# First layer's down projection in four pairs of column chunks, nine seven-product couples each, with GpSimd making the weights' sums

## The chip, the cores and the metric

The kernel runs on one core of a Trainium2 chip. The metric is device time in microseconds: 2390.53 us, the median of 3 runs (2390.34 to 2392.72). Engines are named as in the profile: PE (TensorE matmuls), PEld (its weight loads), DVE (VectorE), ACT (ScalarE), POOL (GpSimd), SP (SyncE, whose queue issues nearly all DMAs).

## The reference

A two-layer encoder over 256 tokens of width 2048. Each layer is a token mixer and then a gated MLP; each has an RMS norm ahead of it and is added to the residual. All is float32.

```python
h = x
for layer in range(2):
    h = h + mixer[layer](rmsnorm(h, g_mix[layer]))          # mLSTM, then HGRN2
    h = h + conv_glu(rmsnorm(h, g_ffn[layer]), ...)
return rmsnorm(h, final_g)

def conv_glu(hn, w_up, conv_w, conv_b, w_down):
    a, v = jnp.split(hn @ w_up, 2, axis=-1)                 # 2048 -> 2 x 5504
    c = conv_b + sum(pad(a)[:, j:j + s] * conv_w[j] for j in range(3))
    return (gelu(c) * v) @ w_down                           # 5504 -> 2048
```

The change is in the last line, `@ w_down`: 43 tiles of 128 rows (k-tiles) times 2048 columns, for 256 tokens.

## The kernel before

**Precision.** Each float32 operand is split into a rounded part (ACT casts, L137) and a rest (DVE subtracts, L138), and a product of two blocks is three matmuls: high by high, high by low, low by high (`product`, L234).

**The order.** One list of chunks is worked through by `stream`. `split_weights` yields pieces of split weights, three ahead of the matmuls (`LOOK`). Raw weights arrive in three buffers of 1 MB (`RAW`), split ones lie in four (`WB`). A scheduler with a timeline of its own then orders the instructions of each engine; DMAs sent through `late` stay in program order on SP's queue. `side` runs small jobs beside the matmuls, by a count of modelled time (`side.tick`).

**The MLP** (`ffn`) has two parts: 22 k-tiles (FA) and 21 (FB). For each, the up projection is computed first, a chunk of 256 columns per k-tile, and then the down projection of these k-tiles. The 2048 output columns are four chunks of 512. In the first part they go as two pairs of chunks (`pair`, `squares_by_seven`); in the second as one pair (chunks 0, 1) and two ordinary chunks (2, 3; `project`, weights w_d2).

**Couples.** Inside a pair, two k-tiles form a couple: a 2 x 2 block product (token halves by k-tiles, k-tiles by column chunks). An ordinary couple takes 8 block products, 24 matmuls. A seven-product couple (in `SEVEN`) takes 7, or 21 matmuls, by Strassen's scheme in Winograd's form. It needs sums of the tokens, S1 to S4 (`token_sums`, four DVE additions and a split), and sums of the weights, T1 to T4 (`weight_sums`, L174 to 184, one DVE operation of 1024 columns and two of 512). A layer has 7 + 6 + 6 of these couples. The products of all couples collect in eight PSUM banks. After the last seven-product couple `mid` adds four of them to the residual `hm` (six DVE operations, one ACT, two POOL: L553 and L554); after the last couple `done` adds the others.

**Sums made ahead.** For six couples of each pair (`STORED`) the T's are made during the up projection: `prepare` (L573) loads two blocks of 512 KB into the tiles `th` and `tl` (shown as pth, ptl), DVE makes the sums, and two stores of 512 KB put them into a DRAM scratch (`tscr`). In the down projection `split_squares` (L186) loads 768 KB of raw weights (B11, B22, B21) and the two sums (1 MB) and splits all: ACT casts (L137, L209) and DVE subtracts (L138, L210), three of 1024 columns and one of 512. Each high or low part of the T's has one buffer.

Of the kernel before, what the change touches and what calls it, by code (L numbers as in the profile page):

```python
# [8 lines left out]
F32 = mybir.dt.float32  # L9
# [39 lines left out]
SEVEN = (1, 2, 4, 5, 7, 8, 9), (1, 2, 4, 5, 7, 8), (1, 2, 4, 5, 7, 8)  # L49
STORED = (1, 2, 4, 5, 7, 8)  # L50
# [10 lines left out]
def trunk_kernel(ctx, tc, xT, x_d, fg_d, pp_d, cst_d, w_gate, w_first, w_aq, w_ak, w_av, w_ao, w_aout, w_ao2,  # L61
                 w_bq, w_bv, w_bg, w_bout, w_bo2, w_up, w_d0, w_d1, w_d2, out, mscr, tscr):
# [113 lines left out]
    def weight_sums(a, b, T, T_):  # L176

        B22, B21, B12 = a[:, 512:1024], b[:, 0:512], b[:, 512:1024]
        dve.tensor_tensor(T.rearrange("p (a b) -> p a b", a=2), B12.unsqueeze(1).broadcast_to([P, 2, 512]),
                          a.rearrange("p (a b) -> p a b", a=2), ALU.subtract)  # L180
        yield 2.5
        dve.tensor_tensor(T_[:, 0:512], B22, T[:, 0:512], ALU.subtract)
        yield 2.5
        dve.tensor_tensor(T_[:, 512:1024], B21, T_[:, 0:512], ALU.subtract)

    def split_squares(ch, parts):  # L186
# [4 lines left out]
        def raw(u):  # L191
            if u not in raws and u < units:
                raws[u] = load_raw(ch.src, 2048 * u, min(2048 * (u + 1), 1024 * ch.nk) - (512 if u in ch.stored else 0))
                if u in ch.stored:
                    kept[u] = [temporary(ch.pool, "T") for _ in range(2)]
                    for t, src in zip(kept[u], ch.stored[u]):
                        nc.sync.dma_start(t, src)
            return raws.get(u)

        def combine(u):  # L200
            r = raw(u)
            T, T_ = kept[u] if u in kept else (temporary(ch.pool, "T") for _ in range(2))
            if u not in kept:
                for _ in weight_sums(r[:, 0:1024], r[:, 1024:2048], T, T_):
                    pass
# [7 lines left out]
        for u in range(units):  # L213
            r = raw(u)
            if u + 1 in ch.seven and not ch.late:
                combine(u + 1)
            wh, wl = parts(r[:, 0:1024], 1024)
            yield wh, wl, 1
            if u + 1 in ch.seven and ch.late:
                combine(u + 1)  # L220
            if 2 * u + 1 < ch.nk:
                m = 512 if u in ch.seven else 1024
                wh, wl = parts(r[:, 1024:1024 + m], m)
                yield wh, wl, sums.pop(u, None)

    def squares_by_seven(ch, fetch, ready):
# [20 lines left out]
        for u in range(units):  # L247
# [3 lines left out]
            if 2 * u + 1 == ch.nk:  # L251
                x = ch.x(2 * u)
                for ps, t, w in ((C11, 0, 0), (C12, 0, 1), (C21, 1, 0), (C22, 1, 1)):
                    product(ps, half(x, t), block(p[:2], w), True)
                side.tick(2.7)
                break
            fetch()
            q = ready.pop(0)
            x0, x1 = ch.x(2 * u), ch.x(2 * u + 1)
            A11, A21, A12, A22 = half(x0, 0), half(x0, 1), half(x1, 0), half(x1, 1)  # L260
            B11, B22, B21 = block(p[:2], 0), block(p[:2], 1), block(q[:2], 0)
            if u in ch.seven:
                sx, t = ch.sums(u), q[2]
                S1, S3, S2, S4 = ((sx[:, i * P:(i + 1) * P], sx[:, 512 + i * P:512 + (i + 1) * P]) for i in range(4))
                T1, T3, T2, T4 = (block(t[i // 2], i % 2) for i in range(4))
                for i, (ps, x, w) in enumerate(((P1, A11, B11), (C12, S4, B22), (C11, A12, B21), (P5, S1, T1),
                                                (P7, S3, T3), (P6, S2, T2), (C21, A22, T4))):
                    product(ps, x, w, u == last and ps in psm_)
                    side.tick(0.65)
# [4 lines left out]
            for ps, (x, w), (y, v) in ((C11, (A11, B11), (A12, B21)), (C12, (A11, B12), (A12, B22)),  # L274
                                       (C21, (A21, B11), (A22, B21)), (C22, (A21, B12), (A22, B22))):
# [251 lines left out]
    def token_sums(mp, i, a, b, S):  # L527

        sx = mp.tile([P, 1024], F32R, tag=f"sx{i}", name="sx")
# [3 lines left out]
        act.copy(sx[:, 0:512], S)  # L533
        dve.tensor_tensor(sx[:, 512:1024], S, sx[:, 0:512].bitcast(F32), ALU.subtract)
        return sx

    def pair(src, nk, c0, x, sums, norm, seven, late=False):
# [18 lines left out]
        def done(ps):  # L556
            for i in range(4):
                h = part(i // 2, i % 2)
                dve.tensor_tensor(h, h, ps[i], ALU.add)
            if norm is not None:  # L560
                norm.add(c0)
# [11 lines left out]
    def prepare(mp, todo, period, finished):  # L573

        yield 24.0
        for src, dst in todo:
            r, T = ([mp.tile([P, 1024], F32, tag=f"{n}{i}", name=f"p{n}") for i in range(2)] for n in ("th", "tl"))
            for i in range(2):
                late(r[i], src[:, i * 1024:(i + 1) * 1024])
            yield 9.0  # L580
            yield from weight_sums(*r, *T)
            for i in range(2):
                nc.sync.dma_start(dst[i], T[i])
            yield max(1.0, period - 14.0)
# [512 lines left out]
    def ffn(layer, norm, nxt):  # L1097
        stack = ExitStack()
        box = dict(n=3 * len(STORED) * layer)
# [10 lines left out]
        def done_up(f, i, GT, SX, seven):  # L1110
            def go(ps):
# [15 lines left out]
                if i % 2 and i // 2 in seven:  # L1127
                    SX[i // 2] = token_sums(mp, seven.index(i // 2), box["c"], c, avc[:, 0:2 * T])
# [3 lines left out]
        for part, (f0, nf) in enumerate(((0, FA), (FA, FB))):  # L1132
            GT, SX, todo, finished = [], {}, [], []

            def prep(todo=todo, finished=finished, nf=nf):
                if not pairs[0].pool:
                    begin()
                side.push(prepare(box["mp"], todo, (nf * 10.4 - 24.0) / len(todo) - 1.5, finished))

            for i in range(nf):  # L1140
                chunks.append(Chunk("fm", w_up[layer, f0 + i], KT, norm.x, done_up(f0 + i, i, GT, SX, SEVEN[2 * part]),
                                    prep if i == 0 else None,
                                    swap=(2,) if part and i == 0 else (3,) if f0 + i == 1 else (), paced=True))
            def two(src, c0, norm, seven, GT=GT, SX=SX, nf=nf, todo=todo, finished=finished):
                ch = pair(src, nf, c0, lambda k: GT[k], lambda u: SX[u], norm, seven)
                for u in STORED:
# [141 lines left out]
```

## Time and profile before

| | us |
|---|---|
| runs, median of 3 | 2390.53 |
| span of the profiled execution | 2388.5 |
| PE busy | 2372.4 |
| DVE busy | 1944.1 |
| ACT busy | 1298.8 |
| POOL busy | 189.7 |
| moved by DMA | 555.07 MB, mean 232 GB/s |

The profiled execution is one run; its span, first to last instruction, is 2.0 us shorter than the median of the runs. "Busy" for PE overlaps: a matmul starts before the one ahead has ended, so the price of one is read from a row of many. Stages, by the trace: the first layer's first up projection from about 388 to 632 us, two pairs to 745, the second up projection to 978, a pair and two chunks to about 1100, the second mixer to about 1680; the second layer's MLP from there to the end.

### The profile page before, as it was taken

The page shows a single profiled execution, that of the slowest core. Times are in us where ns is not written, and L with a number is a line of the kernel's source. Part 1 is how long each engine was busy: PE and PEld are TensorE (multiplying, and loading weights), DVE is VectorE, ACT ScalarE, POOL GpSimd, SP SyncE. Part 2 cuts the span into 40 slices and gives each one's busy share as a digit, 9 for nine tenths or more (in the row PEclk, how much of TensorE's full clock was granted, in tenths as well). Part 3 has the DMA queues.
Part 4 walks back from the last instruction along what each step waited for, and adds up shares of the span by engine and source line. Part 5 has one row for each costly group of instructions (what it writes and reads, how often), then busy time and mean ns, then how long its engine had stood idle before and what let it go on. Part 6 is the DMA issues. An engine that isn't in the chain of part 4 may idle for free.

```text
span 2388.5 us, 37988 instructions
## 1 busy us (share of the span) xinstructions
PE 2372.4 (99%) x14614; PEld 2030.4 (85%) x14614; DVE 1944.1 (81%) x3221; ACT 1298.8 (54%) x2013; POOL 189.7 (8%) x240
## 2 busy tenths in 40 slices
PE   9999999999999999999999999999999999999998
PEld 7888888888888888888888888888888888888887
DVE  7766687988887888777888888888889888788874
ACT  7655455454564554555555555555555565454563
POOL 0100000000000000001222222220000000000000
PEclk9999999999999999999999999999999999999999
DMA  8654556988787777755554554545798888677774
GB/s 300 201 180 165 183 178 211 333 294 317 269 293 254 251 239 262 273 194 182 173 171 168 175 177 160 177 166 188 258 325 298 298 281 296 231 249 263 249 266 148
DMA packets 98789, 555.07 MB, mean 232 GB/s; under 512 B 11168, under 2 KB 11680, under 8 KB 50736
## 3 DMA queue, kind: packets, MB, share of 16 engines
q1 hardware_dynamic: 96912, 548.64, 65.6%
q0 software_dynamic: 1120, 3.21, 0.7%
q8 instruction: 114, 1.87, 0.3%
q10 hardware_dynamic: 576, 0.79, 0.1%
q14 instruction: 67, 0.55, 0.1%
HBM read 512.69 MB, written 39.91 MB: 231 GB/s over the span
## 4 chain that ended last, share of the span: by engine, by line
PE 98%; DVE 1%; issue 1%; DMA 0%; ACT 0%; SPq 0%; POOLq 0%; POOL 0%
PE mm L328 37%; PE mm L344 23%; PE mm L332 18%; PE pc L237 12%; PE mm L237 5%; PE pn L776 1%; PE py L1034 1%; PE pd L984 1%; PE pz L405 0%; PE pa L984 0%; DMA raw<-in_w_first 0%; PE S L762 0%; DVE tl L210 0%; PE pz L1055 0%; PE pa L1009 0%
## 5 line engine op out<-in xcount | busy, mean ns | idle before, releaser
L328 PE MATMUL mm<-xt,wh 128*128 128x512 f32 x3776 | 1313.4, 394 | 0.0
L137 ACT CAST wh<-raw 128x1024 fp32r<-128x1024 f32 (+1 forms) x846 | 853.5, 1019 | 693.8 <-PE mm L328 237.9
L138 DVE TENSOR_TENSOR wl<-raw,wh 128x1024 fp32r<-128x1024 f32 (+1 forms) x846 | 1004.7, 1195 | 265.1 <-ACT wh L137 257.6
L332 PE MATMUL mm<-xt,wl 128*128 128x256 f32 x3776 | 1045.9, 278 | 0.0
L328 PEld LDWEIGHTS mm<-xt,wh 128*128 128x128 f32 x3776 | 706.2, 188 | 159.4
L332 PEld LDWEIGHTS mm<-xt,wl 128*128 128x128 f32 x3776 | 709.5, 188 | 4.5 <-issue 0.4
L344 PE MATMUL mm<-wh,xt 128*128 128x512 f32 x1024 | 320.5, 391 | 3.0 <-ACT xt L350 1.3
L344 PEld LDWEIGHTS mm<-wh,xt 128*128 128x128 f32 x1024 | 191.4, 188 | 43.3 <-ACT xt L350 1.7
L344 PE MATMUL mm<-wl,xt 128*128 128x512 f32 x512 | 198.2, 391 | 0.0
L237 PE MATMUL pc<-wh,g 128*128 128x512 f32 x508 | 167.2, 389 | 0.0
L355 ACT COPY b<-mm 128x256 f32<-128x256 f32 x236 | 87.4, 370 | 122.9 <-PE mm L332 122.7
L210 DVE TENSOR_TENSOR tl<-T,th 128x1024 fp32r<-128x1024 f32 x88 | 109.9, 1264 | 38.9 <-ACT th L209 36.7
L209 ACT CAST th<-T 128x1024 fp32r<-128x1024 f32 x88 | 92.7, 1054 | 73.6 <-PE mm L237 43.5
L237 PEld LDWEIGHTS pc<-wh,g 128*128 128x128 f32 x508 | 95.4, 188 | 19.9
L344 PEld LDWEIGHTS mm<-wl,xt 128*128 128x128 f32 x512 | 96.2, 188 | 18.9
L553 POOL TENSOR_TENSOR hm<-hm,u 128x512 f32<-128x512 f32 x8 | 10.4, 1302 | 1150.9 <-DVE u L552 1150.9
L237 PE MATMUL pc<-wl,g 128*128 128x512 f32 x254 | 98.9, 389 | 0.0
L344 PE MATMUL mm<-wh,g 128*128 128x512 f32 x308 | 96.6, 392 | 0.0
L237 PE MATMUL mm<-th,sx 128*128 128x512 f32 x264 | 91.9, 390 | 0.0
L356 DVE TENSOR_TENSOR avc<-mm,b 128x256 f32<-128x256 f32 x172 | 72.0, 418 | 14.7 <-ACT b L355 14.7
L361 DVE TENSOR_TENSOR avc<-avc,R 128x256 f32<-128x256 f32 x172 | 71.9, 419 | 1.6
L976 DVE COPY kq<-QK 128x256 f32<-128x256 f32 x224 | 69.7, 336 | 0.0
(260 smaller groups left out, 2476.7 us busy)
## 6 DMA issues: line engine op xcount, KB each, us to landing
raw<-in_w_up SPq DMA_DIRECT2D x172, 1024.0 KB, 5.5
raw<-in_w_d SPq DMA_DIRECT2D x48, 1024.0 KB, 5.0
raw<-in_w_bq SPq DMA_DIRECT2D x48, 1024.0 KB, 4.9
pth<-in_w_d SPq DMA_DIRECT2D x72, 512.0 KB, 6.7
tscr<-ptl SPq DMA_DIRECT2D x72, 512.0 KB, 4.7
T<-tscr SPq DMA_DIRECT2D x72, 512.0 KB, 5.1
raw<-in_w_d SPq DMA_DIRECT2D x36, 768.0 KB, 5.2
raw<-in_w_ao SPq DMA_DIRECT2D x24, 1024.0 KB, 4.8
```

Of the source, the lines that this page charges most:

```text
L137: pin(act.copy(wh[:, :m], r))
L138: pin(dve.tensor_tensor(wl[:, :m], r, wh[:, :m].bitcast(F32), ALU.subtract))
L209: act.copy(th, t)
L210: dve.tensor_tensor(tl, t, th.bitcast(F32), ALU.subtract)
L237: pe.matmul(ps, a, b, start=id(ps) not in begun, stop=stop and i == 2)
L328: pe.matmul(ps[f], wh[:, c:c + P], x, start=k + kk == 0, stop=False)
L332: pe.matmul(ps[f][:, 0:T], wl[:, c:c + P], x[:, 0:T], start=False, stop=k + kk == ch.nk - 1)
L344: pe.matmul(ps[t], x[:, a + t * P:a + (t + 1) * P], w[:, c], start=st and i == 0, stop=sp and i == 2)
L355: act.copy(b, ps[:, T:2 * T])
L356: dve.tensor_tensor(dst, ps[:, 0:T], b, ALU.add)
L361: dve.tensor_tensor(dst, dst, R, ALU.mult)
L976: dve.tensor_copy(m[:, j].rearrange("k (m p j) -> k m p j", p=2, j=h), blocks(z, h, 0, T))
```

## The change

- The first layer's chunks 2 and 3 of the second part become a pair too (weights w_d3 in the pair's layout). The second layer keeps its two ordinary chunks there.
- Seven-product couples: nine in each of the first layer's four pairs (couples 1 to 9), 9, 9 and 7 in the second layer's three: 36 + 25 instead of 19 + 19.
- `prepare` now makes T1, T2 and T3 in place on POOL, three operations of 512 columns, from three of the four blocks (512 KB and 256 KB); it stores 512 KB and 256 KB. All seven-product couples of the MLP are prepared.
- T4 is made in the down projection: POOL subtracts T2 from B21, ACT casts, POOL makes the low part. T3 is loaded beside B21 into the raw buffer, so that one split covers both.
- The products of such a couple are issued as four pieces of 2, 2, 2 and 1 products instead of two pieces.
- `token_sums` casts and splits S4 apart from the rest; in the pairs with nine couples it takes the place of token half 2 of the couple's first k-tile, which a seven-product couple doesn't read.
- In ordinary couples C21 comes before C12; `done` closes column chunk by column chunk.

```diff
-SEVEN = (1, 2, 4, 5, 7, 8, 9), (1, 2, 4, 5, 7, 8), (1, 2, 4, 5, 7, 8)
-STORED = (1, 2, 4, 5, 7, 8)
+SEVEN = tuple(range(1, 10)), (1, 2, 3, 5, 6, 7, 8)
...
+                n = 1536 if u in ch.stored else min(2048, 1024 * ch.nk - 2048 * u)
+                raws[u] = load_raw(ch.src, 2048 * u, 2048 * u + n)
                 if u in ch.stored:
-                    kept[u] = [temporary(ch.pool, "T") for _ in range(2)]
-                    for t, src in zip(kept[u], ch.stored[u]):
-                        nc.sync.dma_start(t, src)
+                    kept[u] = temporary(ch.pool, "T")
+                    nc.sync.dma_start(kept[u], ch.stored[u][:, 0:1024])
+                    nc.sync.dma_start(raws[u][:, 1536:2048], ch.stored[u][:, 1024:1536])
...
+            if u in ch.stored:
+                T4 = ch.pool.tile([P, 512], F32, tag="t4", name="t4")
+                pool.tensor_tensor(T4, r[:, 1024:1536], kept[u][:, 512:1024], ALU.subtract)
             wh, wl = parts(r[:, 0:1024], 1024)
             yield wh, wl, 1
+            if u in ch.stored:
+                th, tl = (ch.pool.tile([P, 1024], F32R, tag=n, name=n) for n in ("th0", "tl0"))
+                act.copy(th, kept[u])
+                dve.tensor_tensor(tl, kept[u], th.bitcast(F32), ALU.subtract)
+                yield th, tl, 0
...
+            if u in ch.stored:
+                th, tl = (ch.pool.tile([P, 512], F32R, tag=n, name=n) for n in ("th1", "tl1"))
+                act.copy(th, T4)
+                pool.tensor_tensor(tl, T4, th.bitcast(F32), ALU.subtract)
+                yield th, tl, 0
...
+            if u in ch.stored:
+                S1, S3, S2, S4 = ch.sums(u)
+                products((P1, A11, B11), (C12, S4, B22))
+                fetch()
+                t = ready.pop(0)
+                products((P5, S1, block(t[:2], 0)), (P6, S2, block(t[:2], 1)))
+                fetch()
+                q = ready.pop(0)
+                products((C11, A12, block(q[:2], 0)), (P7, S3, block(q[:2], 1)))
+                fetch()
+                t = ready.pop(0)
+                products((C21, A22, t[:2]))
...
     def prepare(mp, todo, period, finished):
...
+        yield 20.0
+        load(0)
+        for i, (_, dst) in enumerate(todo):
+            yield period / 2
+            r, b = loaded[i]
+            for out, x, y in ((r[:, 0:512], b, r[:, 0:512]), (b, b, r[:, 512:1024]), (r[:, 512:1024], r[:, 512:1024], r[:, 0:512])):
+                pool.tensor_tensor(out, x, y, ALU.subtract)
+            yield period / 4
+            load(i + 1)
+            yield period / 4
+            nc.sync.dma_start(dst[:, 0:1024], r)
+            nc.sync.dma_start(dst[:, 1024:1536], b)
         finished.append(True)
...
-            chunks.append(two(w_d0[layer][:, f0 * 1024:(f0 + nf) * 1024], 0, nxt if part else None, SEVEN[2 * part]))
+            chunks.append(two(w_d0[layer][:, f0 * 1024:(f0 + nf) * 1024], 0, nxt if part else None))
-                chunks += project(lambda c: w_d2[layer, c % 2], nf, lambda k, GT=GT: GT[k], nxt)[2:]
+            if last:
+                chunks[-1].before = nxt.load
+                chunks += project(lambda c: w_d2[c % 2], nf, lambda k, GT=GT: GT[k], nxt)[2:]
             else:
-                chunks.append(two(w_d1[layer], 2, None, SEVEN[1]))
+                chunks.append(two(w_d3 if part else w_d1[layer], 2, nxt if part else None))
```

117 lines of the change are left out of this document (62 added, 55 removed).

## The prediction, made before the changed kernel was run

> **What bounds the kernel now.** I read the page first: the busy shares, the slices and the chain that ended last.
>
> ```profile
> PE 2372.4 (99%) x14614; PEld 2030.4 (85%) x14614; DVE 1944.1 (81%) x3221; ACT 1298.8 (54%) x2013; POOL 189.7 (8%) x240
> PE   9999999999999999999999999999999999999998
> DVE  7766687988887888777888888888889888788874
> POOL 0100000000000000001222222220000000000000
> GB/s 300 201 180 165 183 178 211 333 294 317 269 293 254 251 239 262 273 194 182 173 171 168 175 177 160 177 166 188 258 325 298 298 281 296 231 249 263 249 266 148
> PE 98%; DVE 1%; issue 1%; DMA 0%; ACT 0%; SPq 0%; POOLq 0%; POOL 0%
> ```
>
> TensorE sets the time: it has no slice below nine tenths but the last, and the chain is 98% TensorE. So a matmul taken out counts in full, as long as the engines that feed it keep up. Next comes DVE. POOL is nearly idle except in slices 19 to 26 (the second mixer). How near the feeders are to their limit is read from the stages, so next the busy time by stage: the up projections (388 to 632, 745 to 978, 1678 to 1922), two pairs of the down projection (632 to 745) and the second mixer (1100 to 1580).
>
> ```profile
> core 0: us, PE busy (x) PEld busy (x) DVE busy (x) ACT busy (x) POOL busy (x), PEclk, DMA share, GB/s
> 388.00:632.00 244.00, 244.00 (x1411) 213.28 (x1410) 213.97 (x360) 127.85 (x191) 0.70 (x1) 1.00 0.82 295
> 632.00:745.00 113.00, 112.69 (x502) 92.94 (x501) 92.20 (x100) 66.07 (x74) 7.08 (x4) 1.00 0.80 283
> 745.00:978.00 233.00, 233.00 (x1343) 203.66 (x1342) 194.33 (x317) 117.78 (x173) 0.01 (x1) 1.00 0.72 248
> 1678.00:1922.00 244.00, 244.00 (x1410) 213.33 (x1410) 214.83 (x363) 127.83 (x191) 0.70 (x1) 1.00 0.83 295
> 1100.00:1580.00 480.00, 476.50 (x4343) 411.27 (x4345) 416.46 (x842) 261.45 (x497) 137.33 (x174) 1.00 0.50 170
> ```
>
> TensorE is never without work in the up projections and almost never in the pairs, DVE is at 82 to 88%, and DMA runs at 283 to 295 GB/s where 333 has been reached.
>
> **What is gained: 69 matmuls.** A seven-product couple has 21 matmuls where an ordinary one has 24. Couples go from 19 + 19 to 36 + 25, so 23 more, and 23 x 3 = 69 matmuls fewer; the two column chunks that become a pair cost the same before (252 matmuls) apart from that. The page's mean of 390 ns overlaps with the next matmul, so the price is read from the chain of waits, where 24 in a row take 5.44 us:
>
> ```profile
> 1027.79 5.44 PE pc L237 x24
> ```
>
> That is 0.2267 us each: 69 x 0.2267 = **-15.6 us**. An ordinary couple is 5.44 us of TensorE, a seven-product couple 21 x 0.2267 = 4.76, a lone last tile (12 matmuls) 2.72.
>
> **What a couple asks of DVE and POOL.** Before, a stored couple had four weight splits on ACT and DVE (three of 1024 columns, one of 512). Now DVE has three of 1024, and POOL makes T4 (512 columns) and its low half (512). Each of these five reads two SBUF operands. How DVE and POOL share is shown where the closing of a pair puts two POOL additions beside DVE's splits (the timeline of both engines: start, duration):
>
> ```profile
> 741.46 1.30 POOL L553 TENSOR_TENSOR hm<-hm,u 128x512 f32<-128x512 f32 x1 [43.77 <-DVE u L552]
> 742.73 2.29 POOL L554 TENSOR_TENSOR hm<-hm,u 128x512 f32<-128x512 f32 x1
> 742.23 1.62 DVE L138 TENSOR_TENSOR wl<-raw,wh 128x1024 fp32r<-128x1024 f32 x1 [0.93 <-ACT wh L137]
> 743.77 0.68 DVE L559 TENSOR_TENSOR hm<-hm,pc 128x512 f32<-128x512 f32 x1
> 744.37 1.72 DVE L138 TENSOR_TENSOR wl<-raw,wh 128x1024 fp32r<-128x1024 f32 x1
> 682.40 2.35 DVE L138 TENSOR_TENSOR wl<-raw,wh 128x1024 fp32r<-128x1024 f32 x2
> 684.67 2.35 DVE L210 TENSOR_TENSOR tl<-T,th 128x1024 fp32r<-128x1024 f32 x2
> ```
>
> They take turns. The DVE split issued at 742.23 ends at 743.85, 1.09 after the first POOL addition's end (742.76); the second POOL addition, issued at 742.73, ends at 745.02, 1.17 after that split; the next split ends at 746.09, 1.07 after the POOL end. Only the addition from PSUM (L559) ran its normal 0.68 beside POOL. Undisturbed, a split costs 1.14 (684.67 - 682.40 = 2.27 for two). So a POOL operation takes 1.17 out of DVE's time, and a POOL-DVE turn is 2.24. A seven-product couple needs 2 x 2.24 + 1.14 = **5.62 us** of this shared time against TensorE's 4.76: 0.86 too much. An ordinary couple needs 2 x 1.14 = 2.28 of its 5.44.
>
> The Trainium skill ("GPSIMD Engine Reference", Performance versus the Vector engine) speaks against the move: it puts work on two inputs at about twice VectorE's time, 4497 ns for 2048 columns. An estimate from that figure is 1.12 us for 512 columns; with it for the 1.17 the sum of the pairs below would be 29.6 - 54 x 2 x 0.05 = 24. The trace has 1.30 alone and 1.17 in turns, and those are used.
>
> How much of the 0.86 TensorE sees depends on what carries over. The planned order of the new program puts the products with T one to two couples behind those with B, so ordinary couples can lend time. I therefore balance whole pairs, with 3.0 for the closing (two POOL turns of 1.17 and one DVE addition of two SBUF operands, 0.69):
>
> ```profile
> L550 DVE TENSOR_TENSOR hm<-hm,u 128x512 f32<-128x512 f32 x8 | 5.5, 688 | 0.2
> ```
>
> - 22 tiles, nine couples (four pairs): 9 x 5.62 + 2 x 2.28 + 3.0 = 58.1 against 9 x 4.76 + 2 x 5.44 = 53.7: +4.4 each, 17.6.
> - 21 tiles, nine couples (two pairs): 50.6 + 2.28 + 1.14 + 3.0 = 57.0 against 42.8 + 5.44 + 2.72 = 51.0: +6.0 each, 12.0.
> - The second layer's last, seven couples, three ordinary, one tile: 50.3 against 52.4: 0.
>
> Sum **+29.6**. Bounds: if each of the three dense stages starts with one couple's 5.62 already done, its first pair loses nothing, 29.6 - 4.4 - 6.0 - 4.4 = 15; if nothing is carried to ordinary couples, 61 x 0.86 = 52. I take 29.6, since such a lead and the gaps that two queues leave in each other work against each other.
>
> **The sums made ahead, in the up projections.** DVE loses one operation of 1.22 and two of 0.68 per prepared couple:
>
> ```profile
> L179 DVE TENSOR_TENSOR ptl<-pth 128x1024 f32<-128x1024 f32 x36 | 44.0, 1223 | 26.5 <-DMA pth<-in_w_d 22.7 <-issue 3.6
> L182 DVE TENSOR_TENSOR ptl<-pth,ptl 128x512 f32<-128x512 f32 x36 | 24.6, 683 | 0.0
> L184 DVE TENSOR_TENSOR ptl<-pth,ptl 128x512 f32<-128x512 f32 x36 | 24.6, 683 | 0.0
> L532 DVE TENSOR_TENSOR avc<-avc 128x128 f32<-128x128 f32 x104 | 30.0, 288 | 2.0
> L534 DVE TENSOR_TENSOR sx<-avc,sx 128x512 fp32r<-128x512 f32 x26 | 17.8, 684 | 0.0
> ```
>
> POOL gains three per couple, 18 couples in a stage: 54 x 1.17 = 63 us. The first layer's first stage: DVE 214.0 - 12 x 2.59 = 183; two more token sums at 4 x 0.29 + 0.68 = 1.84 make 187; with POOL's 63 in turns 250 of 244. Its second stage: 194.3 - 6 x 2.59 + 3 x 1.84 = 184, with 63, 247 of 233. The second layer's first: 251 of 244. Lower bound 0, since DVE's PSUM reads and its pauses overlap POOL; upper bound 6 + 14 + 7 = 27. The nearest stage is the second mixer, where DVE is busy 416 of 480 us with POOL at 137, and TensorE still lost only 3.5 of 480, 0.7%. I take that: 0.7% of 244 + 233 + 244 = **+5**. The fourth stage has 7 couples and costs nothing.
>
> On SP's queue the two stores of each prepared couple now wait for POOL; the loads of the up weights stand behind them. Three raw buffers of 1 MB cover this; each lasts 5.5 us (half a chunk of 11.1: 244 over 22). A POOL triple with its waits takes up to 3 x 2.29 = 6.9 of the 10 or more us per couple, so I price it at nothing; without that cover it would show as raw weights landing late. Bytes: a couple loads 0.75 + 0.75 MB instead of 0.75 + 1, so a nine-couple pair asks 9 x 1.57 + 2 x 1.05 = 16.2 MB in 53.7 us, 302 GB/s, below the 333 reached. The swapped order of C12 and C21 moves no work. At the first layer's end two blocks close together, and eight splits of 0.47 on ACT must be ready 5.5 us into the next chunk: bounds 0 and 3, taken **+1**.
>
> ```profile
> L350 ACT ACTIVATE xt<-pz,pp 128x256 fp32r<-128x256 f32 x48 | 21.1, 474 | 10.2 <-PE pz L405 6.3 <-DVE xt L351 3.8
> ```
>
> Sum against the profiled execution: 2388.5 - 15.6 + 29.6 + 5 + 1 = 2408.5. The runs' median lies 2.0 above that span, so **2410** (own range 2396 to 2436).
>
> **Rivals.** (a) *The gain comes through.* If the shared time of a couple stays under 4.76 + 15.6/61 = 5.02, the time falls. For it: DVE had 0.93 us free ahead of the split at 742.23, the mixer lives with both engines, and the planned order gives slack. Against: five turns add up to 5.62. It gives 2390.5 - 15.6 and a little of the rest, 2377. (b) *POOL starves.* The same engines once behaved otherwise:
>
> ```profile
> 1133.50 2.86 POOL L949 TENSOR_TENSOR QK<-q,G 128x256 f32<-128x256 f32 x1 [8.38 <-DVE G L948]
> 1133.67 0.41 DVE L361 TENSOR_TENSOR z<-z,R 128x256 f32<-128x256 f32 x1
> 1134.01 1.21 DVE L138 TENSOR_TENSOR wl<-raw,wh 128x1024 fp32r<-128x1024 f32 x1
> 1135.15 0.41 DVE L996 TENSOR_TENSOR QK<-QK,G 128x256 f32<-128x256 f32 x1
> L949 POOL TENSOR_TENSOR QK<-q,G x32: 727/780/2859, 1114.6 to 1571.7; 128x256 f32<-128x256 f32 x32
> L209 ACT CAST th<-T 128x1024 fp32r<-128x1024 f32 x88 | 92.7, 1054 | 73.6 <-PE mm L237 43.5 <-PE pc L237 15.9 <-DMA T<-tscr 7.1
> L533 ACT CAST sx<-avc 128x512 fp32r<-128x512 f32 x26 | 16.1, 618 | 10.2 <-DVE avc L532 10.0
> ```
>
> An operation of 0.73 waited through three DVE operations that followed each other without a gap. Then ACT, which cannot cast T4 before POOL has made it, holds up the casts behind it, and a couple is a loop: cast T4 0.62, cast B 1.05, three splits 3.41, POOL 1.17 = 6.25, or 1.49 over. By pairs: 4 x 10.1 + 2 x 11.7 + 2.4 = 66, which gives 2390.5 - 15.6 + 66 + 6 = 2447. It decides from the point where DVE has no gap. The Trainium skill ("SBUF — State Buffer", Who interferes with whom) holds that a VectorE instruction with two SBUF inputs and a GpSimd instruction that reads SBUF exclude each other, and that issue order decides who waits; by that order a waiting POOL operation would precede splits issued after it, and (b) could not occur. The turns at 742 agree with it, the row at 1133.50 does not. (c) *It cancels.* The low bound of the pairs, 15, and nothing elsewhere: 2390.
>
> **How the numbers follow.** Forecast 0.47, (a) 0.25, (b) 0.18, (c) 0.10. The measurement can tell 0.2%, 4.8 us, from no change. Faster 0.26 (a and some of c), same 0.08, slower 0.66. Cases of both signs hold weight, so the range runs from 2376, where the gain comes through, to 2446.
>
> **What would show it.** Right: the page has 69 matmuls fewer, DVE's wl and tl in the pairs have means above 1.3 us instead of 1.22, POOL's T4 operations means near 2, TensorE idles inside the pairs behind tl or T4, and four pairs take 57 to 59 us and two about 57. Wrong by (a): TensorE is at 100% in the pairs although these means are up. Wrong by (b): POOL means above 3 and ACT's cast of T4 waiting for POOL. If the up projections lose more than 8 us, the second sum was mis-sized.

## The result, and the profile after

| | before | after |
|---|---|---|
| runs, median | 2390.53 us | 2499.54 us (2496.24 to 2504.01) |
| span of the profiled execution | 2388.5 us | 2495.0 us |

The ratio is 1.0455 (95% interval 1.0442 to 1.0467): 109 us slower, where 2410 was forecast and 2446 was the end of the range. The page of the changed kernel, lines of its busy shares, slices and chain:

```profile
PE 2412.5 (97%) x14545; PEld 2026.0 (81%) x14545; DVE 2108.6 (85%) x3171; ACT 1337.4 (54%) x2101; POOL 735.4 (29%) x547
PE   9999999999889999888999999999999989999998
POOL 0100002333455333453322222220333356411130
PE 67%; DMA 10%; DVE 8%; POOL 7%; issue 6%; ACT 1%; SPq 1%; POOLq 0%; ACTq 0%; DVEq 0%
```

The 69 matmuls are gone (14614 to 14545). But the chain of waits, 98% TensorE before, is now a third DMA, DVE, POOL and queues: TensorE waits for its feeders. The busy time by stage shows where (the first layer's four stages in order, then the second layer's first two; columns as in the prediction):

```profile
core 0: us, PE busy (x) PEld busy (x) DVE busy (x) ACT busy (x) POOL busy (x), PEclk, DMA share, GB/s
390.00:652.00 262.00, 250.59 (x1421) 215.38 (x1419) 236.69 (x340) 126.30 (x198) 93.95 (x55) 1.00 0.76 279
652.00:776.00 124.00, 110.99 (x462) 84.15 (x461) 102.05 (x86) 72.94 (x87) 68.46 (x37) 1.00 0.76 263
776.00:1020.00 244.00, 241.35 (x1358) 208.19 (x1358) 230.54 (x319) 117.64 (x181) 94.15 (x54) 1.00 0.79 288
1020.00:1157.00 137.00, 118.84 (x464) 89.09 (x462) 112.98 (x96) 80.30 (x101) 70.21 (x41) 0.94 0.74 262
1748.00:2009.00 261.00, 253.13 (x1424) 217.46 (x1422) 237.62 (x341) 126.90 (x199) 94.03 (x55) 0.99 0.76 280
2009.00:2131.00 122.00, 110.40 (x459) 83.59 (x458) 100.72 (x85) 71.99 (x86) 69.31 (x37) 1.00 0.76 265
```

An up projection that took 244 us takes 262, two pairs that took 113 take 124, and no engine is full: in the pairs DVE is busy 102 of 124 us, POOL 68, DMA moves 263 GB/s.

Since products of a pair also run at the ends of the neighbouring stages, lengths of stages mix up the causes. So from here on each run is measured by its **gaps**: the time from the start of one matmul to the start of the next, less 0.2267 us (512 columns) or 0.1167 (256), summed over a stage. "Up" is the four up projections, "pairs" the four stretches of pairs, "rest" all else. A level of some 20 us (changes of shape, the kernel's start) is in every run; the differences count.

| run | us | up | pairs | rest |
|---|---|---|---|---|
| before | 2390.5 | 10.6 | 1.5 | 9.5 |
| after | 2499.5 | 55.3 | 75.4 | 12.7 |
| T1 to T3 on DVE | 2468.6 | 20.7 | 80.6 | 14.2 |
| T4 on DVE | 2469.9 | 53.8 | 50.8 | 11.8 |
| all sums on DVE | 2433.9 | 22.1 | 48.3 | 9.8 |
| stores on POOL's queue | 2456.9 | 27.4 | 64.5 | 12.2 |

The sum: from before to after the gaps grow by 44.7 + 73.9 + 3.2 = 121.8; less the 15.6 of the matmuls that is 106.2, and the spans differ by 106.5. All runs below but two were executed once, and the changed kernel's own five executions span 8 us; so a difference of a few us between two runs is weak evidence, and is called so where it is used.

**The up projections.** What ACT's casts waited for in the first of these stages, after:

```profile
ACT wh L136 <- DMA raw<-in_w_up: 54.6, 25, 4.8
```

and in the same stage before:

```profile
ACT wh L137 <- DMA raw<-in_w_up: 4.5, 3, 2.3
```

The up weights land late. Rows from the timeline of SP, POOL and ACT around one prepared couple say why (start, duration, operation, idle before):

```profile
498.94 0.90 SPq L391 DMA_DIRECT2D ptl<-in_w_d  x2
499.89 0.67 SPq L391 DMA_DIRECT2D raw<-in_w_up  x1
506.47 5.09 POOL L621 TENSOR_TENSOR ptl<-ptl 128x512 f32<-128x512 f32 x3 [9.62 <-DMA ptl<-in_w_d]
508.90 1.05 ACT L136 CAST wh<-raw 128x1024 fp32r<-128x1024 f32 x1 [2.68 <-DMA raw<-in_w_up]
510.21 0.33 SPq L626 DMA_DIRECT2D tscr<-ptl  x1
510.64 0.38 SPq L391 DMA_DIRECT2D raw<-in_w_up  x1
```

SP sends the couple's load at 498.94 and one load of up weights, and then stands for almost ten microseconds at the store of that same couple: the load takes 7.5 us to POOL's start, two of POOL's three operations and the start of the store 3.7 more. The next load of up weights is behind the store and leaves at 510.64. Over the whole run these two waits of SP add up to 430 us:

```profile
SPq L626 <- POOL ptl L621: 219.1, 30, 11.4
SPq L626 <- POOL pth L621: 211.1, 31, 10.6
```

**The pairs.** Groups of the first two pairs (652 to 776; busy, mean ns, then the idle time before them and what ended it):

```profile
L137 DVE TENSOR_TENSOR wl<-raw,wh 128x1024 fp32r<-128x1024 f32 x46 | 66.0, 1469 | 18.7 <-ACT wh L136 18.7
L136 ACT CAST wh<-raw 128x1024 fp32r<-128x1024 f32 x45 | 45.6, 1047 | 34.8 <-DMA raw<-in_w_d 30.2 <-DMA raw<-in_w_up 2.3 <-PE pc L244 1.4
L230 POOL TENSOR_TENSOR tl<-t,th 128x512 fp32r<-128x512 f32 x17 | 33.3, 1960 | 45.0 <-ACT th L229 45.0
L213 POOL TENSOR_TENSOR t<-raw,T 128x512 f32<-128x512 f32 x18 | 31.6, 1756 | 11.8 <-DMA T<-tscr 6.7 <-issue 3.8
L219 DVE TENSOR_TENSOR tl<-T,th 128x1024 fp32r<-128x1024 f32 x17 | 27.1, 1595 | 1.7 <-DMA raw<-in_w_d 1.7
```

The splits are longer (1469 and 1595 ns, where the same pairs had 1250 and 1300 before) and POOL's operations take 1.76 and 1.96 us, as announced. But DVE stands idle 18.7 us for ACT's casts, and these 30.2 us for raw weights. One round, from the timeline:

```profile
683.88 2.15 POOL L213 TENSOR_TENSOR t<-raw,T 128x512 f32<-128x512 f32 x1
686.06 0.33 SPq L128 DMA_DIRECT2D raw<-in_w_d  x1
...
692.18 2.00 ACT L136 CAST wh<-raw 128x1024 fp32r<-128x1024 f32 x2 [3.23 <-DMA raw<-in_w_d]
...
694.09 1.04 ACT L218 CAST th<-T 128x1024 fp32r<-128x1024 f32 x1
695.03 0.62 ACT L229 CAST th<-t 128x512 fp32r<-128x512 f32 x1
...
695.73 2.18 POOL L230 TENSOR_TENSOR tl<-t,th 128x512 fp32r<-128x512 f32 x1 [3.16 <-ACT th L229]
...
697.98 1.29 POOL L213 TENSOR_TENSOR t<-raw,T 128x512 f32<-128x512 f32 x1
...
699.29 0.33 SPq L128 DMA_DIRECT2D raw<-in_w_d  x1
```

POOL's T4 at 683.88 is the last reader of a raw buffer; 0.03 us after its end the next raw load leaves. It is cast 6.1 us later, then T's and T4's casts follow (to 695.65), POOL's low part, the next T4, and with its end, at 699.27, the next load in this ring leaves: 13.2 us. Raw blocks are cast two couples ahead of their T4, so of three raw buffers two are held and two couples share such a round: 6.6 us per couple, where TensorE needs 4.76. The rows show the round, not yet that it is what sets the pace; that is tried below.

### The profile page after: what moved, and what is told of

It is laid out like the page before. It is cut to its first block, busy times and chain, and to the rows that moved or that the text cites. A ratio compares the mean times of both kernels' runs of the same rounds, so it can differ in the third digit from the quotient of the medians.

```text
span 2495.0 us, 38564 instructions
## 1 busy us (share of the span) xinstructions
PE 2412.5 (97%) x14545; PEld 2026.0 (81%) x14545; DVE 2108.6 (85%) x3171; ACT 1337.4 (54%) x2101; POOL 735.4 (29%) x547
## 4 chain that ended last, share of the span: by engine, by line
PE 67%; DMA 10%; DVE 8%; POOL 7%; issue 6%; ACT 1%; SPq 1%; POOLq 0%; ACTq 0%; DVEq 0%
PE mm L353 25%; PE mm L369 19%; PE mm L357 13%; PE pc L244 4%; DVE wl L137 4%; DMA raw<-in_w_up 3%; POOL tl L230 2%; POOL t L213 2%; PE mm L244 2%; DMA pth<-in_w_d 2%; DMA ptl<-in_w_d 1%; DMA raw<-in_w_d 1%; DMA T<-tscr 1%; ACT wh L136 1%; POOL ptl L621 1%
## 5 line engine op out<-in xcount | busy, mean ns | idle before, releaser
L137 DVE TENSOR_TENSOR wl<-raw,wh 128x1024 fp32r<-128x1024 f32 (+1 forms) x845 | 1117.4, 1331 | 269.3 <-ACT wh L136 261.4
L353 PE MATMUL mm<-xt,wh 128*128 128x512 f32 x3776 | 1330.1, 397 | 2.0 <-DVE hm L580 1.5
L136 ACT CAST wh<-raw 128x1024 fp32r<-128x1024 f32 (+1 forms) x845 | 869.1, 1037 | 666.5 <-PE mm L353 136.9
L357 PE MATMUL mm<-xt,wl 128*128 128x256 f32 x3776 | 1058.2, 282 | 21.9 <-DVE wl L137 21.4
L621 POOL TENSOR_TENSOR pth<-pth 128x512 f32<-128x512 f32 x93 | 168.5, 1811 | 339.6 <-DMA pth<-in_w_d 334.8
L621 POOL TENSOR_TENSOR ptl<-ptl 128x512 f32<-128x512 f32 x90 | 150.4, 1671 | 275.3 <-DMA ptl<-in_w_d 269.4
L230 POOL TENSOR_TENSOR tl<-t,th 128x512 fp32r<-128x512 f32 x61 | 116.7, 1914 | 170.5 <-ACT th L229 168.9
L213 POOL TENSOR_TENSOR t<-raw,T 128x512 f32<-128x512 f32 x61 | 108.4, 1777 | 32.8 <-DMA T<-tscr 24.7
L529 POOL TENSOR_TENSOR rs<-rs,mhalf 128x2 f32<-128x2 f32 x24 | 16.6, 696 | 318.7 <-DVE rs L528 318.7
L219 DVE TENSOR_TENSOR tl<-T,th 128x1024 fp32r<-128x1024 f32 x61 | 99.1, 1625 | 10.6 <-ACT th L218 8.5
L1163 ACT ACTIVATE avc<-avc 128x256 f32<-128x256 f32 x86 | 35.9, 418 | 125.1 <-DVE avc L1162 125.0
```

The source lines that it names most:

```text
L136: pin(act.copy(wh[:, :m], r))
L137: pin(dve.tensor_tensor(wl[:, :m], r, wh[:, :m].bitcast(F32), ALU.subtract))
L213: pool.tensor_tensor(T4, r[:, 1024:1536], kept[u][:, 512:1024], ALU.subtract)
L219: dve.tensor_tensor(tl, kept[u], th.bitcast(F32), ALU.subtract)
L230: pool.tensor_tensor(tl, T4, th.bitcast(F32), ALU.subtract)
L353: pe.matmul(ps[f], wh[:, c:c + P], x, start=k + kk == 0, stop=False)
```

## The experiments

**Who pays for what: the sums put back on DVE, by parts.**

```diff
e1:  -                pool.tensor_tensor(out, x, y, ALU.subtract)                              # T1 to T3, prepare
     +                dve.tensor_tensor(out, x, y, ALU.subtract)
e2:  -                pool.tensor_tensor(T4, r[:, 1024:1536], kept[u][:, 512:1024], ALU.subtract)
     +                dve.tensor_tensor(T4, r[:, 1024:1536], kept[u][:, 512:1024], ALU.subtract)
     -                pool.tensor_tensor(tl, T4, th.bitcast(F32), ALU.subtract)
     +                dve.tensor_tensor(tl, T4, th.bitcast(F32), ALU.subtract)
e3:  both
```

> The changed kernel with T1 to T3 made by DVE instead of POOL, in place, in the up projections; T4 stays on POOL. Both theories expect the up projections back near the times of before (first 245.6 and 233.0 us, now 262.3 and 244.5): the turn-taking theory because POOL no longer takes DVE's time, the queue theory because SP's stores wait for a shorter producer. DVE is then at about 187 + 18 x 2.05 = 224 of 244 us. The pairs should stay where they are (124 and 137 us in the first layer). Total about 2499 - 51 = 2448; above 2470 would mean that the up projections lose to something else, the added DMAs for instance.

> The changed kernel with T4's sum and low part on DVE instead of POOL; the sums made ahead stay on POOL. Turn-taking theory: a couple asks 3 x 1.14 + 2 x 0.60 = 4.6 us of DVE, under TensorE's 4.76, so the first layer's pairs fall from 124 to about 108 and from 137 to about 107 us. Ring theory (the raw buffer is held until POOL has read it for T4, behind T4's low part, and the next load follows): the same, since DVE frees it. The up projections stay at about 262 and 244. Total about 2499 - 60 = 2440. If the pairs stay above 118, neither is right.

> All four weight sums on VectorE, nothing of the change left on GpSimd. If what the two engines take from each other were the whole loss in the pairs (the prediction's 5.62 us of a couple), it is gone: VectorE needs 3 x 1.14 + 2 x 0.68 = 4.8 of a couple's 4.76, and the time is 2376 to 2395. If half of the pairs' loss comes from the ring of three raw buffers (a buffer is held until T4 has been made from it, two couples after it was loaded), the up projections give back their 35 us and the pairs only the 25 us that the run with T4 on VectorE showed: 2430 to 2440.

Measured: 2468.6, 2469.9 and 2433.9 (table above). T1 to T3 on DVE takes 34.6 us of gaps from the up projections; the first of them is back at its old length with DVE at 216 of 246 us:

```profile
392.00:638.00 246.00, 246.00 (x1424) 215.20 (x1423) 216.37 (x392) 127.25 (x198) 0.70 (x1) 1.00 0.86 299
```

T4 on DVE takes 24.6 us from the pairs (32.3 if T1 to T3 are on DVE already: 80.6 to 48.3). With nothing left on POOL, 47 us more than before are still lost in the pairs. Both first runs came out later than expected (2448 and 2440): each had been credited with more than its own part. The second also met its own sign against both theories: the first layer's pairs stay at 118 and some 123 us, where 108 and 107 were expected. The third came out as the ring's side had it, 39 us above the upper end (2395) that holds if the turns were all. The bytes are the same in the third run, so the added loads and stores are not what the up projections lost by.

Of the 11.5 us that the up projections still lose over before, 9.4 lie in the two that follow pairs, 4.9 and 4.5. These are not waits: all through both stages a matmul of 512 columns and the one of 256 behind it take 353.3 ns from start to start, where the same stages of the kernel before have 346.7, with TensorE busy without a break to speak of (240.80 of 241 us in the first of the two) and the granted clock at 1.00. Some 650 such couples make 4.3 us in each. Which change of the order or the buffers brings this step was not tried; its cause stays open.

**The queue alone.** The stores of T1 to T3 go out from POOL's own queue; POOL still makes the sums.

```diff
-            nc.sync.dma_start(dst[:, 0:1024], r)
-            nc.sync.dma_start(dst[:, 1024:1536], b)
+            pool.dma_start(dst[:, 0:1024], r)
+            pool.dma_start(dst[:, 1024:1536], b)
```

> The changed kernel with the stores of T1 to T3 issued from POOL's own queue, behind POOL's sums, so that SP's queue never waits for POOL in the up projections. POOL's work, DVE's work and the bytes stay. Queue theory (raw up weights are late because the store ahead of them on SP waits for POOL): up projections back to within 4 us of 245.6 and 233.0, total about 2455. Turn-taking theory (DVE loses too much time to POOL): up projections stay at 255 or more and 240 or more, total above 2480.

Measured: 2456.9, and the up projections' gaps fall from 55.3 to 27.4. The first one is 250 us long, at 296 GB/s in place of 279:

```profile
389.00:639.00 250.00, 247.47 (x1420) 216.28 (x1419) 242.27 (x341) 126.77 (x200) 109.39 (x92) 0.99 0.82 296
```

So 28 us of the up projections' loss are SP's wait, and with POOL's work itself only 5 are left over the run with all sums on DVE (27.4 against 22.1), few enough to be called small and no more. In this row DVE is busy 242 of 250 us: the turns are there, at the size that the prediction gave them (250 of 244), and cost little.

**What a turn costs, by itself.** The kernel before, with idle POOL work beside the stored couples of the pairs (couple 9 of the first list is made ordinary, for room: 6 matmuls more):

```diff
+                if u in ch.stored:
+                    idle = ch.pool.tile([P, 512], F32, tag="idle", name="idle")
+                    pool.tensor_tensor(idle, th[:, 0:512].bitcast(F32), th[:, 512:1024].bitcast(F32), ALU.subtract)
```

> The kernel before, with two GpSimd subtractions of 512 columns, two SBUF inputs each, put beside every stored couple of the pairs (72 in all); nothing waits for their result. Couple 9 of the first list is ordinary, for room: 6 matmuls more, +1.4 us. It measures by itself what GpSimd's two operations per couple take from VectorE. If they take turns at 1.17 us each, the two pairs at 632 to 745 need 88 of VectorE, 28 for these and 7 for the closings, 123 us of 113: +10 there and at 1922 to 2036, wl and tl means above 1.3 us, and the time is 2405 to 2415. If the price of GpSimd in the changed kernel is that others wait for its results and not the turns, the time stays within 4 us of 2391.

Measured: 2402.2, between the two expectations; the pairs' gaps rise by 10.4, of which up to 3.4 are two stretches at half the clock (last section). In the first two pairs:

```profile
L213 POOL TENSOR_TENSOR idle<-th 128x512 f32<-128x512 f32 x24 | 51.3, 2138 | 287.6 <-ACT th L209 286.9
L138 DVE TENSOR_TENSOR wl<-raw,wh 128x1024 fp32r<-128x1024 f32 x30 | 46.0, 1554 | 1.8 <-ACT wh L137 1.7
L210 DVE TENSOR_TENSOR tl<-T,th 128x1024 fp32r<-128x1024 f32 x22 | 37.2, 1715 | 7.9 <-ACT th L209 7.9
```

The same groups before:

```profile
L138 DVE TENSOR_TENSOR wl<-raw,wh 128x1024 fp32r<-128x1024 f32 x31 | 38.2, 1250 | 5.7 <-ACT wh L137 5.2
L210 DVE TENSOR_TENSOR tl<-T,th 128x1024 fp32r<-128x1024 f32 x24 | 30.6, 1300 | 12.0 <-ACT th L209 11.4
```

With before's means these splits would take 30 x 1.25 + 22 x 1.30 = 66.1; they take 83.2: 17.1 us for 24 POOL operations, 0.71 each, where the prediction took 1.17. The turns are real and were, if anything, priced too high. For the changed kernel's 122 such operations the gaps found here make 10.4 x 122 / 72 = 18 us, an estimate; there, where ACT, the raw buffers and TensorE wait for the results, they cost 25 to 32. Part of that is the clock: with T1 to T3 on DVE it stood at half for 34.1 us ahead of the kernel's tail, with all sums on DVE for 3.4, so up to 15 of the 32 are TensorE running slower after its waits.

**The ring.** First a second T4 buffer in the first layer, then T4 taken from the stored T's two halves, so that no raw buffer is held for it (with POOL and with DVE). In e14 and e15, and in e16, e18 and e20 below, the right T4 is left out: these kernels do not compute the reference, and only show times.

```diff
e5:       -                T4 = ch.pool.tile([P, 512], F32, tag="t4", name="t4")
          +                T4 = ch.pool.tile([P, 512], F32, tag="t4", bufs=ch.t4, name="t4")      # 2 - layer
e15, e14: -                pool.tensor_tensor(T4, r[:, 1024:1536], kept[u][:, 512:1024], ALU.subtract)
          +                pool.tensor_tensor(T4, kept[u][:, 0:512], kept[u][:, 512:1024], ALU.subtract)    # e14: dve
```

> The changed kernel with two buffers for T4 in the first layer (the second keeps one), so that POOL can make the next couple's T4, and free its raw buffer, ahead of this couple's low part. The number of POOL and DVE operations stays. Ring theory: the raw weights arrive in time, a couple falls from 6.7 us to the turn-taking bound of about 5.6, so the first layer's pairs go from 124 to about 113 and from 137 to about 123 us, total about 2475. Turn-taking with starving (rival b): POOL still waits for DVE's gaps, pairs stay at 6.2 us or more per couple, total above 2490.

> The same one operand in the changed kernel itself: T4 from the two halves of the stored T, all else as it is, on GpSimd. The output leaves out the right T4. If the loop load, casts, low part and T4 on GpSimd, next load (13.2 us for two couples) sets the pairs' pace, it is broken here and the pairs fall from 6.7 us per couple towards the 5.6 of the shared time: 2499.5 - 61 x 0.6 = 2463, with the up projections unchanged. If GpSimd's results or the turns set the pace, 2490 or more.

> As the run with all sums on VectorE, but T4 is taken from the two halves of the stored T and not from the raw block, so that a raw buffer is free as soon as its two casts and splits are done; the engines' work is the same. The output leaves out the right T4. If the raw buffer held for T4 is what the casts wait for (23.2 us of ACT's waits in the first two pairs), most of the 49 us that the pairs still lose goes: 2433.9 - 30 = 2404, at least below 2415. If VectorE, with 4.8 of a couple's 4.76 us, is the limit, or T's own buffers, it stays at 2428 to 2436.

Measured: 2504.2, 2480.9 and 2421.8. The second T4 buffer gained nothing, where 2475 was expected of the ring: SP's waits in the first two pairs moved from one buffer to the others. After, and then with two T4 buffers:

```profile
SPq L194 <- DVE tl L219: 36.8, 14, 4.7
SPq L128 <- POOL t L213: 22.8, 10, 4.5
SPq L128 <- DVE wl L137: 18.2, 10, 6.5
```

```profile
SPq L194 <- DVE tl L219: 38.8, 15, 4.7
SPq L128 <- DVE wl L137: 29.0, 13, 7.0
SPq L128 <- POOL t L213: 8.0, 6, 2.1
```

T's own three buffers (L194 waits for the split of an older T) hold as hard as raw's. Not holding raw for T4 takes 12.8 us of gaps from the pairs with POOL (75.4 to 62.6) and 14.0 with DVE (48.3 to 34.3). So the ring of raw buffers is a cause, but of a fifth of the changed kernel's loss in the pairs, not of most of it; both times fall between their two expectations, short of the gain.

**More buffers.** Couple 9 made ordinary in the six pairs of nine makes room; then a second T4 and a fourth T buffer in the first layer, with POOL, with DVE, and each also with T4 from the stored T.

```diff
e9:  -SEVEN = tuple(range(1, 10)), (1, 2, 3, 5, 6, 7, 8)
     +SEVEN = tuple(range(1, 9)), (1, 2, 3, 5, 6, 7, 8)
e10: also, in layer 0, bufs=TEMP + 1 for the T's and bufs=2 for T4;  e11: e10 with e3's edits
e18: e10 with e15's edit;  e16: e11 with e14's edit
```

> Couple 9 made an ordinary one in the six pairs of nine; GpSimd as in the changed kernel. This is the control for the next run. TensorE gets 6 x 3 x 0.2267 = 4.1 us more, each seven-product couple less saves about 74 / 61 = 1.2 us of waiting in the pairs and 0.7 in the up projections: 2499.5 + 4.1 - 6 x 1.9 = 2492 by either theory, 2485 to 2500.

> As the eight-couple control, with the room of the ninth couple's sums used in the first layer for a second T4 buffer and a fourth T buffer; the engines' work is the same. If the pairs wait because buffers come free late (raw held for T4, T held for its cast), the first layer's four pairs lose 15 us or less in place of about 47 and the time is 2455 to 2470. If they wait because VectorE and GpSimd are short of time on the operands, buffers change nothing: 2485 or more. If only one of two rings opens, it lies between.

> Eight couples, all weight sums on VectorE, and in the first layer the second T4 buffer and the fourth T buffer. From the run with all sums on VectorE (2433.9): +4.1 us for the matmuls, about -5 for six couples fewer. If late buffers are what is left of the loss (34 us in the first layer's pairs by the gaps between matmuls), 25 of it goes: 2408. If not, 2428 to 2436.

> Eight couples, all sums on VectorE, in the first layer a second T4 buffer and a fourth T buffer, and T4 from the two halves of the stored T, so that no raw buffer is held for it. The output leaves out the right T4. If late buffers in two rings are what remains, the gaps of the first layer's four pairs fall from 17 us (10.8 and 6.6 with the room alone) to 8 or less, those of the second layer's first two pairs from 16 to about 10 (the raw ring alone), and the time is 2422.9 - 15 = 2408. If VectorE without slack is what remains, the first layer keeps 14 us or more and the time is 2416 to 2423.

> The same with the sums on GpSimd as in the change. The output leaves out the right T4. With both rings open in the first layer its pairs (20.9 and 19.0 us of gaps with the room alone) keep only what the turns on the operands and the wait for GpSimd's results cost. By the prediction's sum for eight couples, 0.5 us a pair of 22 tiles and 2 of 21, that is 5 us in all: 2462 - 30 = 2432. If GpSimd's results come late in their own right, in order behind ACT's casts, 25 us or more stays: 2445 to 2460.

Measured, with the gaps of the first layer's four pairs and, as the control without the room, of the second layer's first two:

| run | us | first layer | second layer |
|---|---|---|---|
| eight couples (e9) | 2479.2 | 46.8 | 17.5 |
| with room (e10) | 2462.1 | 39.9 | 19.6 |
| and raw not held (e18) | 2450.5 | 35.8 | 13.3 |
| all on DVE, nine couples (e3) | 2433.9 | 34.0 | 14.3 |
| eight couples, with room (e11) | 2422.9 | 17.4 | 16.3 |
| and raw not held (e16) | 2419.9 | 18.6 | 7.8 |

With DVE the room halves the first layer's loss (34.0 to 17.4) while the second layer, which also has a couple less per pair but no room, stays. So late buffers are a cause here too; the room is two buffers at once, and as the second T4 buffer alone gained nothing, the T's are taken to be the ones. Holding raw then matters no more there (18.6), and e16 came out where VectorE without slack was expected (2416 to 2423), which the next run tries.

With POOL both together leave 35.8 of 46.8, and e18 came out where late results were expected (2445 to 2460), the sum of the turns (2432) being far below it. That is 17 us more than with DVE. At the rate found with idle work, 10.4 us for 72 operations, the turns of these four pairs' 64 operations are an estimated 9 of them; how the rest parts into late results and the clock is not shown.

Two times do not mean what they seem to. Eight couples by themselves, expected at 2492, gave 2479.2: the ninth couple of a pair cost about 4 us of waits apiece against the 0.7 us of matmuls that it saves, over half of that in the up projections. And e10 lies in the range expected of open buffers, but its first layer keeps 39.9 us of gaps and not 15; most of its gain over e9, about 12 us, is in the up projections.

**What is left on DVE.** From e16, T4's three operations are taken away too; VectorE then needs 3.4 of a couple's 4.76 us.

```diff
-                th, tl = (ch.pool.tile([P, 512], F32R, tag=n, name=n) for n in ("th1", "tl1"))
-                act.copy(th, T4)
-                dve.tensor_tensor(tl, T4, th.bitcast(F32), ALU.subtract)
+                th, tl = first_t[0][:, 512:1024], first_t[1][:, 512:1024]
                 yield th, tl, 0
```

> As the run with both rings open, without T4's sum, cast and low part: the last product of a couple takes the second half of the stored T in its place, and its output is not the reference's. VectorE needs 3 x 1.14 = 3.4 of a couple's 4.76 us and ACT 3.2. If VectorE's time is what the four pairs still lose by, their gaps fall from 18.6 us to 6 or less and the time is 2419.9 - 20 = 2400 or less, the second layer's pairs included. If ACT's casts wait for the single th buffers, 14 us or more stays there and the time is above 2410.

Measured: 2414.0; the four pairs keep 16.2 of 18.6 us, and the second layer's first two rise from 7.8 to 12.4. So it isn't VectorE's time. What ACT's casts wait for in the first two pairs of this run:

```profile
ACT th L215 <- PE pc L240: 36.1, 12, 5.5
...
ACT wh L136 <- DMA raw<-in_w_d: 5.1, 4, 1.7
```

They wait for TensorE to let go of the one `th` buffer, and all later casts wait behind them in order. That fits the remaining 16 us, but a second `th` buffer (8 KB with its low part) had no room and wasn't tried; this run holds `th` one product longer; and in the kernel before ACT's casts of the T's waited 20.1 us for TensorE in these pairs (13.5 and 6.6) without a loss; so this part is argued, not shown.

**The part that pays.** The kernel before with only the fourth pair (e12: its six stored couples as in the other pairs, sums by DVE), and with couple 9 in all lists as well (e19).

```diff
e12: -                chunks += project(lambda c: w_d2[layer, c % 2], nf, lambda k, GT=GT: GT[k], nxt)[2:]
     +            if part and layer:
     ...
     +                chunks += project(lambda c: w_d2[c % 2], nf, lambda k, GT=GT: GT[k], nxt)[2:]
                  else:
     -                chunks.append(two(w_d1[layer], 2, None, SEVEN[1]))
     +                chunks.append(two(w_d3 if part else w_d1[layer], 2, nxt if part else None, SEVEN[2 * part if part else 1]))
e19: +SEVEN = ((1, 2, 4, 5, 7, 8, 9),) * 3
```

> Of the change only the fourth pair: the kernel before, with the first layer's last two column chunks made a pair with its six stored couples; sums made by VectorE and stored whole, as before. 18 matmuls fewer are 4.1 us. VectorE in the up projections before it: 194 + 6 x 2.59 = 210 of 233 us. If a pair of six couples is fed without loss as the three others are, the time is 2386 (ratio 0.998); if the end of the layer, where two blocks now close together, costs what the change's closing was taken for, 1 to 3 us of that is lost: 2387 to 2390.

> The kernel before with the fourth pair and couple 9 added to every pair's list (its sums made in the pair by VectorE, as in the first list of before): 5 couples more than the run with the fourth pair alone, 15 matmuls or 3.4 us. VectorE gets about 2.59 us more in a pair of 53 in which it was busy 47. If it is fed, 2388.6 - 3.4 = 2385; if a pair of 21 tiles with seven couples begins to wait, 2387 to 2392.

Measured: e12 2388.58 us against 2390.95 on the same chip, ratio 0.9985 (0.9976 to 0.9994), pairs' gaps 1.9; 2.4 us of the 4.1, the rest going where the layer ends (rest 11.3 in place of 9.5). It is the fastest version here, by 0.15%.

e19 is 1.003 (1.0019 to 1.0042), 2397.2 us and above both of its expectations: 15 matmuls fewer, but gaps of 19.4 + 4.0 + 11.1 in place of 10.6 + 1.9 + 11.3. The pairs wait only 2.1 us more, less than the 3.4 that the matmuls save. What makes it slower are the 8.8 us in the up projections, and these are the even step found above. The second up projection in e12 and then in e19, TensorE busy throughout in both, with 18 matmuls fewer in 1 us more:

```profile
748.00:981.00 233.00, 233.00 (x1345) 203.65 (x1345) 206.06 (x335) 117.95 (x175) 0.00 (x0) 1.00 0.84 304
748.00:982.00 234.00, 234.00 (x1327) 202.92 (x1326) 209.12 (x340) 117.21 (x173) 3.57 (x2) 1.00 0.83 295
```

So e19 does not show that a seventh couple costs a pair more than it brings.

## Why the prediction was wrong

- **What bounds, and the gain.** Right: TensorE was the bound, and 69 matmuls fewer are 15.6 us by the balance of gaps and spans.
- **"On SP's queue ... I price it at nothing."** The step that failed in the up projections. It put POOL's triple (6.9 us) against the 10 us of a couple, and three raw buffers against that. But the store waits for the triple, and the triple for its load, 7.5 us: the two in a row are 11.3 us of one couple, and SP stands through most of them. What the text named as the sign ("raw weights landing late") is what came: 28 us.
- **Turns in the up projections, +5.** Borne out: 5 us by the run with the stores elsewhere, DVE 242 of 250; a difference of that size between two runs executed once says that the turns are cheap, not more. The sign that the prediction gave, up projections losing more than 8 us, came (44.7), mostly by the queue and not by the turns.
- **Turn-taking in the pairs, +29.6.** The size came out, in part by luck: putting T4 on DVE gives back 25 to 32, but a bare turn costs 0.71 and not 1.17, an estimated 18 us in all; the rest is waiting for POOL's results and the clock after such waits. The pairs took 62 us each (124 for two), not the 57 to 59 announced.
- **"I therefore balance whole pairs."** The step that failed in the pairs. A balance of busy times assumes that any engine can work ahead. Here a couple is a round through a load (6.1 us), ACT, POOL and a buffer that is freed last of all, and the prediction has no term for it. With no work on POOL at all the pairs still lose 47 us: 14 from raw buffers held for T4, some 17 in the first layer from T's buffers (the two don't add up), and about as much that stays open. The 302 GB/s that it asks for was not reached either (263 in the first two pairs); what the rows show there is casts waiting for single loads.
- **End of the first layer, +1.** Inside its bounds: 1.8 in the run with the fourth pair alone.
- **A reading.** "DMA runs at 283 to 295 GB/s" leaves out the second up projection, 248 in the same rows; no term rests on it.
- **Rivals.** (a) and (c) fell. (b), 2447, was nearest in time, but not by its mechanism: ACT's cast of T4 waited for POOL 4.0 us in the whole run, POOL for that cast 168.9:

```profile
POOL tl L230 <- ACT th L229: 168.9, 60, 9.3
...
ACT th L229 <- POOL t L213: 4.0, 6, 2.4
```

The terms as measured: 2388.5 - 15.6 + 28 (SP's queue) + 5 (turns, up) + 12 (up projections with nothing on POOL, some 9 of them the even step, cause open) + 25 (POOL in the pairs) + 49 (buffers and order, a third of it open) + 3 (rest) = 2495. The losses from the clock are inside these terms.

## What to carry to other kernels

Before a piece of work goes to a slower engine, follow its result and not its busy time: who stands in which queue until it is there, and what is behind that in the queue; a store of a late result belongs in the queue of the engine that makes it. For a stage in which every stretch is alike, write down the round of each buffer (load, readers, last reader, next load) and divide by the number of buffers that are really free; if that is longer than the bound's own time, spare time on the engines doesn't help.

## What the runs showed of the hardware that was not expected

TensorE's clock falls to half after short waits and makes them dearer. In stretches of 3.4 us of the changed kernel:

```profile
690.30:693.70 3.40, 1.90 (x9) 1.26 (x8) 0.44 (x1) 1.52 (x2) 2.19 (x2) 1.00 0.75 231
...
1082.60:1086.00 3.40, 1.03 (x5) 0.67 (x4) 1.52 (x2) 1.87 (x2) 0.00 (x0) 1.00 1.00 396
...
1086.00:1090.00 4.00, 4.00 (x12) 3.00 (x11) 3.95 (x4) 2.54 (x4) 3.20 (x2) 0.58 1.03 385
```

After a stretch with TensorE at 1.90 of 3.40 us the clock stays; after one at 1.03 the next 3.41 us run at half (0.58 over 4 us), matmuls of 512 columns starting 0.43 us apart. The longest wait in that stretch was 2.37 us. Another, at 1092.80, had TensorE busy for 1.74 us and was followed by half the clock too. Before the tail this happens six times, for 27.3 us in all, so up to 13.7 us of the changed kernel's gaps are the clock and not the wait itself; in the kernel before there is none. The Trainium skill ("TensorE: Matmul & The Clock Gate", Part 1) puts this down to a free-running window of 3413 ns and half the clock after an idle window; the trace agrees with the window, but here one with TensorE at work for a third of it was enough. The clock does not explain the 8 us between the changed kernel's executions: 2496.24 and 2504.01 us both had a mean of 0.994.

Matmuls can also step more slowly without any wait and at the full granted clock: 353.3 ns instead of 346.7 for one of 512 columns and one of 256, through the whole of an up projection. The kernel with the fourth pair alone and the one with couple 9 added differ by that couple only, and the second steps slowly in both up projections that follow pairs.
